# A written order for ScalarE, VectorE and GpSimd in a two-pair delta-rule scan, with its steps rearranged and two transfers on GpSimd's queue

## The chip, the cores and the metric

The kernel runs on one core of one Trainium2 chip. The metric is the device time of one execution in microseconds (us); the median of three runs of the kernel before is 2773.27 us. One execution was also taken by the hardware profiler, and its page and trace are what is read here. Engines: PE is TensorE's matmul side, PEld its weight loads, DVE is VectorE, ACT is ScalarE, POOL is GpSimd, SP is SyncE, which issues most transfers (DMAs).

## The reference

A two-layer decoder with a model width of 2048 and 272 tokens (16 learned meta tokens ahead of 256). Layer 0 is an RWKV-7 time mix followed by a SwiGLU; layer 1 is stick-breaking attention followed by a SwiGLU. The change touches the time mix alone, which has 32 heads of 64 channels:

```
r, k, v = xr @ w_r, xk @ w_k, xv @ w_v           # x* = h mixed with the token before
decay = exp(-exp(w)),  w from tanh(xw @ dec_w1) @ dec_w2
a = sigmoid(a_w0 + (xa @ a_w1) @ a_w2)
g = sigmoid(xg @ g_w1) @ g_w2
kk = k * k_k;  kk = kk / |kk| per head
k = k * (1 + (a - 1) * k_a)
for each token t, per head:
    sa    = state @ (-kk_t)
    state = state * d_t + sa (kk_t * a_t)^T + v_t k_t^T
    y_t   = state @ r_t
y = (y - mean) * rsqrt(var + GN_EPS) * gn_w + gn_b  # per head
out = ((y + sum(r * k * r_k) * v) * g) @ w_o
```

## The kernel before, in words

**Pairs and chunks.** Two heads fill the 128 partitions, so there are 16 head pairs (`Pair`). Tokens are cut into a chunk of 16 (meta) and four chunks of 64. In a chunk the recurrence becomes matrix products with the inverse of a unit triangular matrix. That inverse is made in three levels: the 16x16 diagonal blocks by substitution on GpSimd (`solve`, tiles As and Ts), then blocks of 32 (`left(16)`, `right(16)`), then of 64 (`left(32)`, `right(32)`). A level transposes the inverse so far (Tt into Tn, VectorE), multiplies it with the strict blocks (An times Tt into the bank yb, PE), masks that into Ys (VectorE), multiplies with Tn into the bank zb (PE, L1418) and adds zb into Tt (VectorE, L1422).

**The scan.** `scan` handles two pairs at a time and runs three stages of different pairs in one step d. A (pairs 2d, 2d+1) goes through the states: `states` and `update` (bank cb, L1470 and L1493), `output`, the group norm (`square`, `variance`, `log`, `norm`) and `gate` (bank gp, output o). B, the next two pairs, goes through `chunk0`, `scores`, `bonus`, `tokens`, the inverse, `values` (banks kv and k0), `apply` (tiles wa, X, Ah) and `trans` (bank rm). C, the two after, is prepared: `lora` makes the decays and keys (ld, L, P, Q, kk and the products AR, ARV, BK, B0), rk is the product for the bonus, and `negatives` makes the strict blocks (`neg`: bank b, tiles An and An0), sends them through DRAM scratch (s1, `diagonals`) into As and starts the solve. The step after stores Ts to scratch s2 and loads it back as Tt (`inverse`). Steps run from d = -2 to 7; d = 0 to 5 are alike and hold A, B and C. In d = 6 there is no C, in d = 7 neither B nor C.

**Fills.** Between the stages `f(k)` runs k accumulation steps of the projections w_r, w_v and, at the end, w_o. Such a step is three matmuls, since weights and activations are split in a high and a low part (`mm3k`, L200 to L202). The weight parts are made by ScalarE (whi, L228) and VectorE (wlo, L229), three pieces of four steps ahead. They are what keeps PE at work while the chains of the scan run on the other engines.

**What sets the order.** PE and SP run in the order in which the program is written. ScalarE, VectorE and GpSimd are ordered by a scheduler, but for a few instructions that `keep_in_program_order` holds: the transpose of the first level, the casts of weights and of the gates (`split_gates`, L202's wlo), and the copy in `split_low`.

**Other places that the steps below touch.** `head_sums` (L1193 to L1199) sums a tile over its head: it casts and splits it (tile hs, from rk or sq, the squares) and multiplies with a matrix of ones (vb, bv). The two products of kk with Q (B0, L1262; BK, L1263) are on VectorE, those of k with Q (L1264, L1265) on GpSimd. `load_norm` brings the keys' norms rn from DRAM (rkd), through SyncE's queue, as are all of `diagonals`' stores. rk takes the buffer of Q (`ALIAS`), Ah that of Tn. An0 and sq have one buffer. The norms of half of the keys come late, from `key_norm(1, late)` (L551 on: Ln, Exp and two table loads, L555); it is written behind `negatives` in d = -1, and the scheduler moves it ahead. The loads of h (L964), sixteen of 136 KB, go through GpSimd's queue in the last steps.

Of the kernel before, what the change touches and what calls it, by code (L numbers as in the profile page):

```python
# [11 lines left out]
F32 = mybir.dt.float32  # L12
# [25 lines left out]
ALIAS = {"kk": "ld", "rs20": "L", "rs21": "Q", "rk": "Q", "Ah": "Tn", "Mp": "Ys", "sq": "ta"}  # L38
# [94 lines left out]
class Builder:  # L133
# [240 lines left out]
    def time_mix(self):  # L374
# [15 lines left out]
        with ExitStack() as ctx:  # L390
# [6 lines left out]
            zero = zero.rearrange("p a b c t -> p (a b c t)")[:, :325]  # L397
            nc.gpsimd.memset(zero, 0.0)
            for i in range(2):
# [5 lines left out]
                for n, sides in (("s1", self.s1), ("s2", self.s2)):  # L405
                    z = self.dram.tile([10, 65, 64], F32, name=f"{n}_{i}", tag=f"{n}_{i}", bufs=1)
                    nc.scalar.dma_start(z.rearrange("s i t -> (s i t)").rearrange("(p x) -> p x", p=128),
                                        zero)
                    sides.append(z)
# [255 lines left out]
    def scan(self, sp):  # L665
# [25 lines left out]
        pairs[0].load_norm()  # L691
        for d in range(-2, NK // 2):
            A, B, C, N = two(d), two(d + 1), two(d + 2), two(d + 3)
            f = fill if C else lambda k: fill(k * 7 / 8)
# [892 lines left out]
```

## Time and profile before

| | |
|---|---|
| median of 3 runs | 2773.27 us (2773.12 to 2777.41) |
| profiled execution | 2768.93 us, span 2767.2 us |
| PE busy | 2664.3 us, 96% of the span (21030 matmuls) |
| PEld, DVE, ACT, POOL busy | 2484.6 (90%), 1780.0 (64%), 1468.1 (53%), 144.5 us (5%) |
| moved by DMA | 439.40 MB, 159 GB/s in the mean |
| steps d = 0 to 5 | begin at 245.9, 313.0, 378.7, 446.1, 511.9 and 577.6 us |
| steps d = 6 and 7 | begin at 643.9 and 700.9 us |

Times within the span are counted from its start. An instruction of the trace is shown by its start, its duration, engine, line, operation, output and input tiles, shapes, how many in a row, and in brackets how long its engine stood idle before it and which instruction released it. A group of waits shows the waiting matmul's tile and line, the releasing engine, tile and line, and the total, the count and the longest. A window shows length, busy time (and count) of PE, PEld, DVE, ACT and POOL, then the clock that TensorE was granted as a share of full speed, the busy share of the DMA engines and GB/s. The scan ends at about 760 us; the rest of the span is the feed-forward layers and the attention.

### The profile page before, as it was taken

What the parts mean: (1) busy time and instruction counts of PE and PEld (TensorE: products, weight loads), DVE (VectorE), ACT (ScalarE), POOL (GpSimd) and SP (SyncE); (2) the same over time, 40 slices, a digit from 0 to 9 for tenths busy, and PEclk for the clock granted to TensorE, in tenths of its full rate; (3) what the DMA queues carried; (4) which work ended last, traced back from release to release, by engine and by line L of the source; (5) the groups of instructions that cost most, each with busy time, mean ns of one, the idle gap of its engine ahead of it and who ended that gap; (6) DMA issues with size and microseconds to landing.
All of it is one profiled execution on the core that took longest, in us unless ns stands there. A gap on an engine that the chain in (4) does not pass through costs nothing.

```text
span 2767.2 us, 54183 instructions
## 1 busy us (share of the span) xinstructions
PE 2664.3 (96%) x21030; PEld 2484.6 (90%) x21030; DVE 1780.0 (64%) x3549; ACT 1468.1 (53%) x3030; POOL 144.5 (5%) x357
## 2 busy tenths in 40 slices
PE   9988888888999999999999999999999999999999
PEld 8887777778899999999999999988888888888888
DVE  7666555555665555555555876588776666666665
ACT  7764444444554444444444665477555455455553
POOL 0022222222000000000000000000000000000000
PEclk9999899999999999999999999999999999999999
DMA  6433333334455555555555555533555655655555
GB/s 228 139 113 99 85 92 86 86 89 118 136 175 176 167 185 175 166 186 171 169 184 167 181 171 171 175 123 114 175 186 179 200 189 176 198 189 179 197 180 177
DMA packets 186002, 439.40 MB, mean 159 GB/s; under 512 B 57328, under 2 KB 89232, under 8 KB 185744
## 3 DMA queue, kind: packets, MB, share of 16 engines
q1 hardware_dynamic: 184112, 432.41, 49.5%
q8 instruction: 165, 2.70, 0.4%
q0 software_dynamic: 768, 2.23, 0.3%
q10 hardware_dynamic: 864, 1.29, 0.1%
q14 instruction: 93, 0.76, 0.1%
HBM read 430.28 MB, written 5.58 MB: 158 GB/s over the span
## 4 chain that ended last, share of the span: by engine, by line
PE 87%; DVE 5%; ACT 3%; DMA 2%; issue 2%; POOL 1%; SPq 0%; DVEq 0%; ACTq 0%; POOLq 0%
PE mm L205 22%; PE mm L200 15%; PE mm L202 15%; PE mm L201 15%; PE mm L204 11%; DMA rn<-rkd 1%; PE lr L601 1%; PE mm L502 1%; DVE wlo L229 1%; PE zb L1418 1%; PE cb L1493 1%; PE z L1122 1%; PE lt L1135 0%; PE yb L1402 0%; POOL Tm L848 0%
## 5 line engine op out<-in xcount | busy, mean ns | idle before, releaser
L182 DVE TENSOR_TENSOR wlo<-raw,whi 128x512 fp32r<-128x512 f32 (+1 forms) x1432 | 968.1, 679 | 595.0 <-ACT whi L181 576.6
L181 ACT CAST whi<-raw 128x512 fp32r<-128x512 f32 (+1 forms) x1432 | 870.2, 610 | 841.9 <-PE mm L201 531.4
L200 PE MATMUL mm<-hl,whi 128*128 128x272 f32 x3328 | 968.3, 291 | 1.8 <-ACT hl L271 1.8
L202 PE MATMUL mm<-hl,wlo 128*128 128x272 f32 x3328 | 965.8, 290 | 0.3 <-DVE wlo L229 0.3
L201 PE MATMUL mm<-hl,whi 128*128 128x272 f32 x3328 | 963.3, 289 | 0.0
L205 PE MATMUL mm<-hl,whi 128*128 128x512 f32 x2624 | 919.8, 395 | 0.0
L204 PE MATMUL mm<-hl,wlo 128*128 128x256 f32 x2624 | 739.1, 282 | 0.0
L200 PEld LDWEIGHTS mm<-hl,whi 128*128 128x128 f32 x3328 | 630.3, 189 | 6.4 <-issue 2.8
L201 PEld LDWEIGHTS mm<-hl,whi 128*128 128x128 f32 x3328 | 635.5, 191 | 0.0
L202 PEld LDWEIGHTS mm<-hl,wlo 128*128 128x128 f32 x3328 | 630.5, 189 | 1.0 <-DVE wlo L229 0.7
L205 PEld LDWEIGHTS mm<-hl,whi 128*128 128x128 f32 x2624 | 492.9, 188 | 111.0
L204 PEld LDWEIGHTS mm<-hl,wlo 128*128 128x128 f32 x2624 | 494.9, 189 | 0.3
L229 DVE TENSOR_TENSOR wlo<-raw,whi 128x512 fp32r<-128x512 f32 (+1 forms) x154 | 103.8, 698 | 69.8 <-ACT whi L228 68.8
L228 ACT CAST whi<-raw 128x512 fp32r<-128x512 f32 (+1 forms) x154 | 88.2, 612 | 24.5 <-PE mm L201 14.1
L221 DVE TENSOR_TENSOR h<-h,mm 128x256 f32<-128x256 f32 (+1 forms) x224 | 93.9, 420 | 6.6 <-PE mm L205 6.0
L200 PE MATMUL mm<-hi,whi 128*128 128x272 f32 x256 | 79.4, 310 | 0.0
L214 ACT COPY c<-mm 128x256 f32<-128x256 f32 x104 | 38.8, 373 | 76.0 <-PE mm L205 76.0
L202 PE MATMUL mm<-hi,wlo 128*128 128x272 f32 x256 | 75.2, 294 | 0.3 <-DVE wlo L229 0.3
L201 PE MATMUL mm<-lo,whi 128*128 128x272 f32 x256 | 75.5, 295 | 0.0
L1418 PE MATMUL zb<-Ys,Tn 64*64 64x64 f32 x512 | 24.4, 256 | 42.3 <-DVE Tn L1394 40.9
L1418 PEld LDWEIGHTS zb<-Ys,Tn 64*64 64x64 f32 x512 | 21.7, 167 | 45.2 <-issue 42.3
L200 PEld LDWEIGHTS mm<-hi,whi 128*128 128x128 f32 x256 | 50.2, 196 | 2.9 <-issue 0.6
(301 smaller groups left out, 2427.9 us busy)
## 6 DMA issues: line engine op xcount, KB each, us to landing
raw<-w_gate SPq DMA_DIRECT2D x176, 512.0 KB
raw<-w_up SPq DMA_DIRECT2D x176, 512.0 KB
raw<-w_down SPq DMA_DIRECT2D x128, 512.0 KB
raw<-w_down SPq DMA_DIRECT2D x128, 192.0 KB
raw<-w_r SPq DMA_DIRECT2D x32, 512.0 KB
raw<-w_v SPq DMA_DIRECT2D x32, 512.0 KB
raw<-sb_w_k SPq DMA_DIRECT2D x32, 512.0 KB
raw<-sb_w_v SPq DMA_DIRECT2D x32, 512.0 KB
```

Of the source, the lines that this page charges most:

```text
L181: nc.scalar.copy(hi, part)
L182: nc.vector.tensor_tensor(lo, part, hi.bitcast(F32), ALU.subtract)
L200: mm(out, w[0], x[0], start=first, stop=False)
L201: mm(out, w[0], x[1], start=False, stop=False)
L202: return mm(out, w[1], x[0], start=False, stop=last)
L204: mm(out[:, :n], w[1], x[0], start=first, stop=False, skip_group_check=True)
L205: return mm(out, w[0], x[2], start=False, stop=last, skip_group_check=True)
L214: self.nc.scalar.copy(c, out[:, n:])
L221: self.nc.vector.tensor_tensor(h, h, out[:, c:c + n], ALU.add)
L228: self.cast = nc.scalar.copy(hi, part)
L229: nc.vector.tensor_tensor(lo, part, hi.bitcast(F32), ALU.subtract)
L1418: self.PE.matmul(zb[r, i * 64:i * 64 + 64], self.Tn[r, i], self.Ys[r, i], start=True, stop=True)
```

## The change

**Written order.** From d = -1 on, `in_order` chains every instruction of ScalarE, VectorE and GpSimd to the one written before it on the same engine. Only the splits of the outputs o stay free (`loose`). The calls of `keep_in_program_order` in these parts go.

**The step rearranged.** The numbers of fills between the stages change. B's inverse is fetched ahead of the bonus, and A's squares are summed between bonus and tokens. `lora` is cut in two: `decay` (matmuls, ld, L, ta, k2) stands ahead of the first inverse level, `keys` (P, Q, kk, AR, ARV, BK, B0, rk) behind it. The norm is cut as well: the exponent (`root`) stays early, the rest comes behind the first level, one pair behind `values` and one behind `left(32)`. `gate` moves from ahead of `left(32)` to behind `apply`; `split_gates` stays where it was, some fills ahead of `right(32)`. `negatives` moves four fills behind `right(32)`.

**Engines and queues.** The products of kk with Q go from VectorE to GpSimd, the square in the norm from VectorE to ScalarE, the product of y with the norm from VectorE to GpSimd. `load_norm` and the stores of An0 in `diagonals` go from SyncE's to GpSimd's queue. The scratch tiles s1 and s2 become one each for both pairs, so that one store carries Ts and one load As.

**Banks and buffers.** kv and k0 of the two pairs move from banks 0, 4 and 1, 5 to 0, 2 and 1, 3. yb of `left(32)` lies in banks 0 and 1 where C exists. The norm's factor lies in the tile that becomes o.

The first place is VectorE around the first inverse level of a like step. Before, the keys kk with all their products stand ahead of the transposes Tn, and the adds of zb into Tt come last:

```order
L1238 SCALAR_TENSOR_TENSOR kk<-kt,vecs,rn 128x272
L1274 TENSOR_TENSOR AR_5375<-mm,P 128x16
L1258 SCALAR_TENSOR_TENSOR AR_5375<-kk,P 128x16
L1259 SCALAR_TENSOR_TENSOR ARV<-kk,P 128x4x64
L1275 TENSOR_TENSOR ARV<-mm,P 128x4x64
L1261 SCALAR_TENSOR_TENSOR kk<-ta,kk 128x272
L229 TENSOR_TENSOR wlo<-raw,whi 128x512
L1262 TENSOR_TENSOR B_0_2017<-kk,Q 128x16
L1263 TENSOR_TENSOR BK<-kk,Q 128x2x2x64
L1394 STREAM_TRANSPOSE Tn<-Tt 128x256 x2
L1278 SCALAR_TENSOR_TENSOR rk<-mm,dv,k_5368 128x272
L1422 TENSOR_TENSOR Tt<-Tt,zb 128x256
```

The same place after; the second pair's transpose and its masked product Ys now come first, and the keys stand between them and the two adds:

```order
L1436 STREAM_TRANSPOSE Tn<-Tt 128x256
L1445 TENSOR_TENSOR Ys<-yb,consts 128x256
L1280 SCALAR_TENSOR_TENSOR kk<-kt,vecs,rn 128x272
L1300 SCALAR_TENSOR_TENSOR AR_6272<-kk,P 128x16
L1301 SCALAR_TENSOR_TENSOR ARV<-kk,P 128x4x64
L1303 SCALAR_TENSOR_TENSOR kk<-ta,kk 128x272
L1316 TENSOR_TENSOR AR_6272<-mm,P 128x16
L1317 TENSOR_TENSOR ARV<-mm,P 128x4x64
L1320 SCALAR_TENSOR_TENSOR rk<-mm,dv,k_6220 128x272
L1231 TENSOR_TENSOR hs<-rk,hs 128x272
L229 TENSOR_TENSOR wlo<-raw,whi 128x512
L1460 TENSOR_TENSOR Tt<-Tt,zb 128x256 x2
```

What moved: the transposes from behind the keys to ahead of them, the two products of kk with Q away from VectorE, and rk, the split of hs and a weight split to ahead of the adds.

The second place is ScalarE behind `neg`, where An is the copy of the strict 64x64 blocks and An0 (16x16) that of the meta chunk. Before:

```order
L1335 COPY An<-b_5718 128x128
L1335 COPY An<-b_5719 128x128
L1338 COPY An_5733<-b_5718 16x16 x2
L1335 COPY An<-b_5737 128x128
L1335 COPY An<-b_5736 128x128
L1198 CAST hs<-rk 128x272
L1338 COPY An_5751<-b_5736 16x16 x2
L228 CAST whi<-raw 128x512 x2
L1442 COPY X<-wa 64x2x128 x4
L228 CAST whi<-raw 128x512 x4
```

After, in the same stretch:

```order
L1377 COPY An<-b_5687 128x128
L1377 COPY An<-b_5688 128x128
L1380 COPY An_5702<-b_5687 16x16 x2
L1377 COPY An<-b_5705 128x128
L1377 COPY An<-b_5706 128x128
L1380 COPY An_5720<-b_5705 16x16 x2
L228 CAST whi<-raw 128x512 x2
L1480 COPY X<-wa 64x2x128 x4
L1230 CAST hs<-rk 128x272
L228 CAST whi<-raw 128x512 x4
```

What moved: the cast of rk, which stood ahead of the second pair's An0, now stands behind it and behind the copies X; the rest reads alike, but it is now fixed, so nothing passes a copy that waits.

The third place is GpSimd in the same step, where B is the part of a product for the meta chunk, BK that for the others, and the numbered k is k2. Before, the copy into Ts and the products of both pairs stand ahead of the first step of the solve (Tm, the last row), and no transfer is among them:

```order
L844 COPY Ts<-consts 80x256
L1234 TENSOR_SCALAR k_6258<-ta,vecs,dv 128x272
L1235 TENSOR_TENSOR k_6258<-k_6258,kt 128x272
L1264 TENSOR_TENSOR B_0_2017<-k_6258,Q 128x16
L1265 TENSOR_TENSOR BK<-k_6258,Q 128x2x128
L1234 TENSOR_SCALAR k_6438<-ta,vecs,dv 128x272
L1235 TENSOR_TENSOR k_6438<-k_6438,kt 128x272
L1264 TENSOR_TENSOR B_1_2027<-k_6438,Q 128x16
L1265 TENSOR_TENSOR BK<-k_6438,Q 128x2x128
L848 TENSOR_TENSOR Tm<-Ts,As 80x15
```

After, from the second pair's products to the copy into Ts with which the solve begins:

```order
L1304 TENSOR_TENSOR B_1_2025<-k_5528,Q 128x16
L1305 TENSOR_TENSOR BK<-k_5528,Q 128x2x128
L1306 TENSOR_TENSOR B_1_2025<-kk,Q 128x16
L1307 TENSOR_TENSOR BK<-kk,Q 128x2x2x64
L1560 TENSOR_TENSOR y<-y,o 128x272
L1236 DMA rn<-rkd 128x1x272
L867 DMA s_2015<-An_5702 16x16 x2
L867 DMA s_2015<-An_5720 16x16 x2
L875 COPY Ts<-consts 80x256
```

What moved here: L1306, L1307 and L1560 came from VectorE, the three rows of DMA from SyncE; they stand ahead of the solve.

The diff, cut to its core:

```diff
-            self.s1 = []
-            self.s2 = []
+            self.s1, self.s2 = (self.dram.tile([20, 65, 64], F32, name=n, tag=n, bufs=1)
+                                for n in ("s1", "s2"))
...
+            if d == -1:
+                mark = traced[-1]
...
             for x in B:
                 x.scores()
-            f(6 if A else 2)
+            if B:
+                self.inverse(B)
+            f(1)
             for x in B:
                 x.bonus()
+            for x in A:
+                x.square()
+            f(2 if A else 1)
             for x in B:
                 x.tokens()
-            if B:
-                self.inverse(B)
-            for x in A:
-                x.square()
+            f(4 if A else 1)
             for x in A:
                 x.variance()
             for x in A:
                 x.log()
             for x in A:
-                x.norm()
+                x.root()
+            f(3)
+            if C:
+                C[0].decay(2, 3)
+            f(3)
+            for x in B:
+                x.left(16)
+            if C:
+                C[0].keys()
+                C[1].load_norm()
+            f(6)
+            for x in B:
+                x.right(16)
+            f(2)
+            for x in B:
+                x.values()
+            if A:
+                A[0].norm()
+                if not C:
+                    A[1].norm()
             f(4)
             if C:
-                C[0].lora(2, 3)
+                C[1].decay(2, 3)
             f(4)
             for x in B:
-                x.left(16)
-            f(5)
-            for x in B:
-                x.right(16)
-            for x in B:
-                x.values()
+                x.left(32, bool(C))
             if C:
-                C[1].load_norm()
-            f(5)
-            if C:
-                C[1].lora(2, 3)
-            f(5)
+                C[1].keys()
+                if A:
+                    A[1].norm()
+                if N:
+                    self.load_low(N)
+                    N[0].load_norm()
+            f(3)
             self.split_gates(gates, A)
             f(4)
-            for x in A:
-                x.gate()
-            for x in B:
-                x.left(32)
-            f(7)
             for x in B:
                 x.right(32)
+            f(4)
             if C:
                 self.negatives(C)
             if d == -1:
                 key_norm(1, late)
-            f(8)
+            f(5)
             for x in B:
                 x.apply()
-            if N:
-                self.load_low(N)
-                N[0].load_norm()
-            f(8)
+            f(3)
+            for x in A:
+                x.gate()
+            f(5)
             for x in B:
                 x.trans()
-            f(8)
+            f(11)
+        self.in_order(traced, mark)
         fill(100)
...
+    def in_order(self, traced, mark):
+        start = next(k for k, i in enumerate(traced) if i is mark) + 1
+        kinds = mybir.EngineType
+        prev = {}
+        for i in list(traced[start:]):
+            if i.engine not in (kinds.Activation, kinds.DVE, kinds.Pool) or i.name in self.loose:
+                continue
+            if i.engine in prev:
+                self.tc.add_manual_dep(
+                    i, prev[i.engine].name,
+                    mybir.DependencyInfo(mybir.DependencyClass.NoSync, mybir.DependencyReason.DATA),
+                    reason="order")
+            prev[i.engine] = i
...
-                self.dq.dma_start(s1[r, 0:META, 4, 0:META], x.An0[HS[r]][:META])
-        for i, x in enumerate(two):
-            self.dq.dma_start(self.As[i * 40:i * 40 + 40], x.diag(self.s1[i]))
+                self.nc.gpsimd.dma_start(s1[r, 0:META, 4, 0:META], x.An0[HS[r]][:META])
+        self.dq.dma_start(self.As, Pair.diag(self.s1))
...
-        for i, x in enumerate(two):
-            self.dq.dma_start(x.diag(self.s2[i]), self.Ts[i * 40:i * 40 + 40])
+        self.dq.dma_start(Pair.diag(self.s2), self.Ts)
...
-        self.nc.sync.dma_start(self.rn, self.b.rkd[2 * self.p:2 * self.p + 2].unsqueeze(1).to_broadcast([2, 64, T]))
+        self.nc.gpsimd.dma_start(self.rn, self.b.rkd[2 * self.p:2 * self.p + 2].unsqueeze(1).to_broadcast([2, 64, T]))
...
-        V.tensor_tensor(self.B0[:, 0:META], kk[:, :META], Q[:, :META], ALU.mult)
-        V.tensor_tensor(par(BK, 0, 1), c4(kk), c4(Q), ALU.mult)
         E.tensor_tensor(self.B0[:, 32:32 + META], k2[:, :META], Q[:, :META], ALU.mult)
         E.tensor_tensor(par(BK, 1, 0), c4(k2), c4(Q), ALU.mult)
+        E.tensor_tensor(self.B0[:, 0:META], kk[:, :META], Q[:, :META], ALU.mult)
+        E.tensor_tensor(par(BK, 0, 1), c4(kk), c4(Q), ALU.mult)
...
-        kv = self.bank("kv", 0, 4)
-        k0 = self.bank("k0", 1, 5)
+        kv = self.bank("kv", 0, 2)
+        k0 = self.bank("k0", 1, 3)
...
-        if s == 16:
-            b.tc.keep_in_program_order(op)
-            yb = self.bank("yb", 0, 1)
-        else:
-            yb = self.bank("yb", 4, 5)
+        yb = self.bank("yb", 0, 1) if low else self.bank("yb", 4, 5)
...
     def log(self):
-        self.rs2 = self.t272(f"rs2{self.e}")
-        self.A.activation(self.rs2, self.vb, AF.Ln, bias=self.b.gneps)
+        self.out = self.b.kp.tile([128, T], F32, name="o", tag="kp")
+        self.A.activation(self.out, self.vb, AF.Ln, bias=self.b.gneps)
+
+    def root(self):
+        self.A.activation(self.out, self.out, AF.Exp, scale=-0.5)
 
     def norm(self):
...
-        V.tensor_tensor(sq, rs2, rs2, ALU.mult)
+        self.A.activation(sq, rs2, AF.Square)
         V.scalar_tensor_tensor(sq, vb, GN_EPS, sq, ALU.add, ALU.mult)
         V.scalar_tensor_tensor(rs2, sq, -3.0, rs2, ALU.add, ALU.mult)
-        V.tensor_tensor(y, y, rs2, ALU.mult)
-        V.scalar_tensor_tensor(y, y, self.vec("mgn"), self.bv, ALU.mult, ALU.add)
+        self.nc.gpsimd.tensor_tensor(y, y, rs2, ALU.mult)
...
     def gate(self):
         b = self.b
         w = self.wg
+        self.V.scalar_tensor_tensor(self.y, self.y, self.vec("mgn"), self.bv, ALU.mult, ALU.add)
```

More of the change, by code (lines that the diff above doesn't have):

```diff
@@ L37 @@
 CONST = {}
-ALIAS = {"kk": "ld", "rs20": "L", "rs21": "Q", "rk": "Q", "Ah": "Tn", "Mp": "Ys", "sq": "ta"}
+ALIAS = {"kk": "ld", "rk": "Q", "Ah": "Tn", "Mp": "Ys", "sq": "ta"}
 NRAW = 4
@@ L404, in time_mix @@
                 self.static.append(st)
[L405 to L409, printed above, removed]
+            for z in (self.s1, self.s2):
+                nc.scalar.dma_start(z.rearrange("s i t -> (s i t)").rearrange("(p x) -> p x", p=128),
+                                    zero)
             self.blk = [sp.tile([128, 128], F32R, name="blk", tag=f"blk{i}") for i in range(2)]
@@ L801, in split_low @@
         l = self.l2.tile([128, 512], F32R, name="w2l", tag="w2l", bufs=1)
-        self.tc.keep_in_program_order(self.nc.scalar.copy(h, self.low))
+        self.nc.scalar.copy(h, self.low)
         self.nc.vector.tensor_tensor(l, self.low, h.bitcast(F32), ALU.subtract)
@@ L819, in split_gates @@
         h, l = self.whl_pair(w)
-        self.tc.keep_in_program_order(self.cast)
         for i, x in enumerate(two):
@@ L1221, in lora, with keys @@
         V.tensor_tensor_scan(L, b.cst("reset"), ld, 0.0, ALU.mult, ALU.add)
-        ta = self.t272("ta")
+        self.L = L
+        self.ta = ta = self.t272("ta")
         A.activation(ta, za[:, :T], AF.Tanh, bias=self.vec("ha0"), scale=0.5)
+        self.k2 = k2 = self.t272("k2")
+        E.tensor_scalar(k2, ta, self.vec("k_a"), self.vec("oka"), ALU.mult, ALU.add)
+        E.tensor_tensor(k2, k2, kt, ALU.mult)
+    def keys(self):
+        b, p, V, A, nc = self.b, self.p, self.V, self.A, self.nc
+        E = LORA(nc)
+        kt, rn, L, ta, k2 = b.k[p], self.rn, self.L, self.ta, self.k2
         self.P = P = b.P
@@ L1386, in values, with left @@
         A.copy(self.KV0, k0[:, 0:64])
-    def left(self, s):
+    def left(self, s, low=True):
         b, V, PE = self.b, self.V, self.PE
```

24 lines of the change are left out of this document (13 added, 11 removed).

## The prediction

> **What bounds the kernel now.** I read the windows by stage first. In each the columns are the length, then the busy time and count of PE, its weight loads, VectorE, ScalarE and GpSimd, then the granted TensorE clock, DMA share and GB/s.
>
> ```profile
> 900.00:1000.00 100.00, 100.00 (x799) 100.00 (x798) 56.47 (x98) 43.44 (x76) 0.00 (x0) 1.00 0.54 175
> 446.00:512.00 66.00, 54.53 (x732) 50.14 (x732) 36.66 (x90) 30.66 (x82) 16.75 (x42) 0.92 0.34 90
> 644.00:701.00 57.00, 49.76 (x656) 45.60 (x654) 31.51 (x77) 25.11 (x61) 10.93 (x33) 0.91 0.38 119
> ```
>
> From 760 us on PE never stops and the change touches nothing there. In the scan PE is idle for 11 of 66 us and its clock falls. The other engines are half idle, so they are late, not full. Next come PE's own waits (total, times, longest), and the ends of one step.
>
> ```profile
> PE zb L1418 <- DVE Tn L1394: 40.9, 6, 6.9
> PE gp L202 <- DVE wlo L229: 18.3, 6, 3.7
> PE gp L200 <- ACT whi L228: 3.5, 6, 0.6
> ...
> 445.75 0.29 PE L201 MATMUL mm<-hl,whi 128*128 128x272 f32 x1
> 445.88 0.29 PE L202 MATMUL mm<-hl,wlo 128*128 128x272 f32 x1
> 446.10 0.29 PE L1470 MATMUL cb<-SC,WV 64*64 64x16 f32 x4
> ...
> 475.95 0.37 PE L1418 MATMUL zb<-Ys,Tn 64*64 64x64 f32 x2 [6.89 <-DVE Tn L1394]
> ...
> 511.94 0.29 PE L1470 MATMUL cb<-SC,WV 64*64 64x16 f32 x4
> ```
>
> Six like steps, 65.84 us each (446.10 to 511.94). In each PE waits 6.8 us at `right(16)` for the transposes and 0.6 + 3.05 us in `gate` for the gates' split: 10.45 us. A filling matmul takes 0.125 us, start to start. I count from a step's start; PE reaches the first wait at 22.96 (475.95 - 6.89 - 446.10). Behind each wait the clock falls:
>
> ```profile
> 476.00:478.00 2.00, 2.00 (x50) 2.00 (x52) 1.41 (x5) 0.94 (x2) 0.00 (x0) 0.50 0.03 8
> 478.00:480.00 2.00, 2.00 (x35) 1.88 (x32) 1.49 (x4) 1.51 (x5) 0.00 (x0) 0.50 0.23 45
> ...
> 490.00:492.00 2.00, 2.00 (x10) 1.93 (x10) 1.49 (x3) 0.00 (x0) 0.00 (x0) 0.59 0.75 256
> 492.00:494.00 2.00, 2.00 (x40) 1.82 (x40) 0.93 (x3) 0.00 (x0) 0.00 (x0) 0.56 0.65 203
> ```
>
> PE is busy at half clock for 4 us, then at 0.59 and 0.56 for 4: lost work of 2.0 + 1.7 = 3.7 us. A step without these waits would take 65.84 - 10.45 - 3.7 = 51.7.
>
> **Term 1, the first inverse level (faster).** VectorE's rows, then ScalarE's:
>
> ```profile
> 470.77 0.29 DVE L1220 TENSOR_SCALAR ld<-ld 128x272 f32<-128x272 f32 x1
> 470.98 0.41 DVE L1407 TENSOR_TENSOR Ys<-yb,consts 128x256 f32<-128x256 f32 x1
> 471.31 0.71 DVE L1221 TENSOR_TENSOR_SCAN L<-consts,ld 128x272 f32<-128x272 f32 x1
> ...
> 475.37 0.76 DVE L1394 STREAM_TRANSPOSE Tn<-Tt 128x256 f32<-128x256 f32 x2
> 476.06 0.45 DVE L1278 SCALAR_TENSOR_TENSOR rk<-mm,dv,k 128x272 f32<-128x272 f32 x1
> 477.10 0.42 DVE L1422 TENSOR_TENSOR Tt<-Tt,zb 128x256 f32<-128x256 f32 x1 [0.59 <-PE zb L1418]
> 477.44 0.44 DVE L1199 TENSOR_TENSOR hs<-rk,hs 128x272 fp32r<-128x272 f32 x1
> 477.79 0.68 DVE L229 TENSOR_TENSOR wlo<-raw,whi 128x512 fp32r<-128x512 f32 x1
> ```
> ```profile
> 460.22 0.65 ACT L1364 COPY G<-tb 128x256 f32<-128x256 f32 x2
> 460.75 0.43 ACT L1198 CAST hs<-sq 128x272 fp32r<-128x272 f32 x1
> 461.26 0.59 ACT L1367 COPY X<-tv 128x512 f32<-128x512 f32 x1
> 461.87 1.28 ACT L1510 ACT_TABLE_LOAD   x1
> ...
> 466.50 0.48 ACT L1219 ACTIVATE ld<-zw,dv 128x272 f32<-128x272 f32 x1
> ```
>
> VectorE holds the whole norm and the keys ahead of the transposes. The change puts both behind them; the second norm square goes to ScalarE, the product with y to GpSimd. Now `ld` gates everything. The bonus stands 15 fills (1.9 us) earlier, so the second `hs` cast starts at 460.75 - 446.10 - 1.9 = 12.75; behind it come 0.43, all four G and two X copies (2 x 0.65 + 2 x 0.59), a weight cast 0.52 and the 4.63 from table load to `ld`: 20.8, 0.4 later than now. VectorE then has `ld` until 21.3, the rest of a split 0.25, 0.29, 0.71, a split 0.6, and transpose and mask 0.38 + 0.41 for each pair: Ys at 23.95 and 24.7. As many fills lie ahead of `right(16)` as before (57), so PE comes at 22.96 and waits 1.1 us in place of 6.8.
>
> **Term 2, a new wait in `values` (slower).** `kv` and `k0` of the second pair move from banks 4 and 5 to 2 and 3, which hold both pairs' zb. PE may write them only when VectorE has added zb into Tt, and in the written order that add stands behind the keys, rk, hs and a split. Two prices come from here:
>
> ```profile
> 485.25 0.74 POOL L1265 TENSOR_TENSOR BK<-k,Q 128x256 f32<-128x256 f32 x1
> 485.86 0.50 DVE L1238 SCALAR_TENSOR_TENSOR kk<-kt,vecs,rn 128x272 f32<-128x272 f32 x1 [2.11 <-DMA rn<-rkd]
> ...
> 487.02 0.44 DVE L1261 SCALAR_TENSOR_TENSOR kk<-ta,kk 128x272 f32<-128x272 f32 x1
> ```
>
> From 24.7: kk to kk 1.6 (485.86 to 487.46); the two products moved to GpSimd 0.2 + 0.74, for which rk must wait since it takes Q's buffer; rk 0.45; ScalarE's cast 0.43; hs 0.44; the split 0.68; Tt 0.42: 29.7, and 30.1 for the second pair. PE has the second zb, six fills (0.75) and the first pair's kv behind 24.75, some 1.9 us by my estimate (the busy 4 us at half clock above hold both zb and both kv and fills besides), so 26.6. It waits 3.1 + 0.4 = 3.5 us. If my queue is too long by 3 us this is nothing; above, nothing in these rows reaches 6.
>
> **Term 3, the gates and `An0`.** The gates' split now lies long before `gp`: 3.65 us go. A late link comes instead. An0 has one buffer, so ScalarE's copy for the second pair waits until the first pair's stores land, and these leave through GpSimd's queue. In the written order the casts, X copies and rk's cast stand behind that copy.
>
> ```profile
> L964 POOL DMA_DIRECT2D h<-xT x16: 536/536/728, 634.9 to 643.5; - x16
> ...
> DMA to landing us min/median/max: 2.6/4.0/8.3
> ...
> 503.93 0.34 ACT L1338 COPY An<-b 16x16 f32<-16x16 f32 x2
> 504.29 1.14 ACT L228 CAST whi<-raw 128x512 fp32r<-128x512 f32 x2
> ```
>
> Before shows no store on GpSimd's queue. Above stands the slowest load there, 8.3 us; below, SyncE's same store, landed by 503.93. I take 2.6, the quickest load: these stores hold 1 KB. The Trainium skill, "DMA: Bandwidth & Descriptors" (Anatomy of one DMA), gives this queue a fixed cost of about 2.0 us; by that the sum would be 0.6 us a step better, and no run here shows it yet. From the start of `neg`: An0 at 1.2, second issue at 1.75, landed 4.35; copy 0.34 and two casts 1.14, 5.85; VectorE's split 0.68, two Ah 0.84, AR, ARV and rk 0.95, 8.3; cast and hs 0.87; then y, o, y, o at some 0.47: 11.0. `trans` needs gp's banks 4 and 5, so it waits for both o. PE has neg 1.1, wa 1.96, 39 fills 4.9 and gp 1.5: 9.5. Wait 1.5 us.
>
> **Term 4, the clock.** The wait of 3.5 us is about as long as those at the gates, so I charge a half-clock spell of 1.75. For 1.5 us this is near:
>
> ```profile
> 714.57 0.87 PE L1193 MATMUL vb<-hs,blk 128*128 128x272 f32 x2 [2.18 <-ACT hs L1198]
> ...
> 716.00:717.00 1.00, 1.00 (x6) 1.00 (x5) 0.68 (x2) 0.98 (x2) 0.00 (x0) 0.50 0.06 16
> ```
>
> A gap of 2.18 us is followed by half clock, so behind 1.5 us I charge half a spell, 0.9. Here the Trainium skill's page "TensorE: Matmul & The Clock Gate" (Why this matters for your kernels) says otherwise: no drop without an idle gap of over some 3 us. This row differs, so it enters only as a rival.
>
> **Sum of a step.** Gone: 10.45 + 3.7 = 14.15. New: 1.1 + 3.5 + 1.75 + 1.5 + 0.9 = 8.75. A step takes 60.4, that is 5.4 less; six of them 32.4.
>
> **The other steps.** Ahead of the six:
>
> ```profile
> 171.99 1.28 ACT L555 ACT_TABLE_LOAD   x1
> ...
> 181.25 0.72 PE L1328 MATMUL b<-BK,ARV 64*64 64x64 f32 x16 [3.86 <-DVE BK L1263]
> ...
> 658.31 0.74 POOL L1315 COPY Rh<-ARV 128x256 f32<-128x256 f32 x2
> ```
>
> The late key norm (two table loads, 1.28 each, and its Ln) now runs in a scheduled hole at 171.99, and the keys behind it make PE wait 3.86. Written, it stands behind `neg` of the next step: some 3 us saved in one place, some 4.5 spent in the other, where ScalarE's casts and VectorE's Ah queue behind An0 and those loads: -1.5. In the step without new keys (57 us now) the solve ends at 658.31, 14.4 after its start, since sixteen loads of h stand ahead of it on GpSimd; that stays. PE will come earlier to `left(16)` and wait there for Tt, so of its gaps some 4 us go and no more. At the end the product with y adds a hop through GpSimd: -1. The single store of Ts, the single load of As, and rn on GpSimd's queue I cost at nothing: the solve's 12 us and the six fills ahead of `keys` cover them; without that cover each would cost an issue, 0.54.
>
> Together 32.4 - 1.5 + 4 - 1 = 33.9. The profiled execution took 2768.93 (span 2767.2): 2735 by it. The median of the three runs is 4.3 higher, 2773.27, so I forecast 2739.
>
> **Rivals.**
>
> The clock stays up behind the short waits, as that page would have it. Each step keeps 1.75 + 0.9 = 2.65, six 15.9: 2723. For it: the first 1.1 us wait is too short to matter. Against: the 2.18 us gap. Chance 0.12.
>
> The new waits don't come: ScalarE and VectorE run ahead of what I strung together, so kv finds Tt added and An0 is not late. Then 3.5 + 1.75 + 1.5 + 0.9 = 7.65 more a step, 46: 2693. For it: both engines are busy half the step. Against: strict order, each link above has its row. Chance 0.15.
>
> GpSimd's stores land at the median of its loads, 4.0: the third term grows by 1.4 and its clock to the full 1.75, 2.3 a step, 14: 2753. Chance 0.13.
>
> **Slower or nothing gained:** they land as its slowest load, at 8.3. ScalarE stands for them, and casts, X, rk, both o and PE's `trans` behind it: 5.7 + 0.9, and 0.5 at `left(16)`, where As comes late too: 7.1 a step, 43: 2782. It cancels the gain at a landing of some 7.3 us. For it: ScalarE can't pass the blocked copy any more, as it did with rk's cast before 503.93. Against: 1 KB against loads of 136 KB, sixteen in flight. Chance 0.20, of which 0.08 end within 0.2% and 0.12 beyond.
>
> That the order isn't obeyed is no rival: the rows of the changed program stand as written.
>
> **How the numbers follow.** Forecast 0.40, the rivals 0.12, 0.15, 0.13 and 0.20. Faster by over 0.2% (5.5 us, about what a measurement of this kernel tells from no change): 0.40 + 0.12 + 0.15 + 0.13 = 0.80; within 0.08; slower 0.12. From 2698 to 2780 lies all but half of the second rival and most of the slow end: some 0.8.
>
> **What would show it.** Right: PE's waits in each step are zb for Ys near 1 us, `kv` for Tt near 3 and `rm` for o near 1.5; gp's wait is gone; steps of some 60 us; a half-clock spell behind kv. Term 2 is wrong if kv shows no wait on Tt; term 3 if rm shows none, or if ScalarE isn't idle before An0's second copy. The whole is wrong if PE waits for weight splits (wlo) in the fills, which I costed at nothing because casts lie three chunks ahead, or for Tt in every step.

## The result, and the profile after

The changed kernel takes 2749.88 us in the median of four runs (2747.76 to 2752.10), against 2773.19 of the kernel before. The ratio is 0.9915, 95% interval 0.9897 to 0.9932: faster by 0.85%, where 2739 us were forecast. The profiled execution took 2748.35 us with a span of 2746.6, so 20.6 us are to be found in the trace.

PE's waits after, in the columns of the list before (total, times, longest):

```profile
PE kv L1419 <- DVE Tt L1460: 18.6, 7, 2.9
PE rm L1489 <- DVE o L1570: 17.4, 12, 2.6
PE cb L1531 <- ACT S L1525: 11.1, 24, 0.6
PE zb L1456 <- DVE Ys L1445: 9.0, 7, 1.3
PE b L1370 <- POOL BK L1307: 6.5, 1, 6.5
PE gp L200 <- ACT An L1380: 6.1, 5, 1.4
```

The waits for Tn (40.9 us) and for the gates' split (21.8 us) are gone, but for 0.5 us. In their place stand the three links that the prediction named, zb and kv in nearly the forecast size and rm at twice it, and one at gp that it did not have. That one comes five times and not six. The waits at cb are not new (9.8 us in 22 before); the one at b lies ahead of the six steps. The like step that began at 446.10 before is this one after:

```profile
442.02 0.29 PE L1508 MATMUL cb<-SC,WV 64*64 64x16 f32 x4
...
466.23 1.34 PE L1456 MATMUL zb<-Ys,Tn 64*64 64x64 f32 x32 [1.28 <-DVE Ys L1445]
...
472.05 0.53 PE L1419 MATMUL kv<-X,G 64*64 64x64 f32 x10 [2.92 <-DVE Tt L1460]
...
493.11 0.39 PE L200 MATMUL gp<-hg0h,whi 128*128 128x272 f32 x1 [1.36 <-ACT An L1380]
...
499.35 0.43 PE L1489 MATMUL rm<-G,Ah 64*64 64x128 f32 x2 [2.59 <-DVE o L1570]
500.36 2.03 PE L1489 MATMUL rm<-G,Ah 64*64 64x128 f32 x30 [0.58 <-DVE o L1570]
508.54 0.29 PE L1508 MATMUL cb<-SC,WV 64*64 64x16 f32 x4
```

It lasts 66.52 us, against 65.84: nothing is gained in it. The starts of all steps give the account:

| stretch | before, us | after, us | gain | forecast |
|---|---|---|---|---|
| up to step 0 | 245.9 | 246.8 | -0.9 | -1.5 |
| steps 0 to 4 | 331.7 | 327.6 | 4.1 | 27.0 |
| step 5 | 66.2 | 60.5 | 5.8 | 5.4 |
| step 6 | 57.0 | 48.6 | 8.4 | 4 |
| step 7 and after | | | 3.2 | -1 |
| all | | | 20.6 | 33.9 |

Step 5 is what was forecast, 60.48 us against 60.4. Steps 0 to 4 take 65.0 to 66.5. Steps 0, 3 and 5 as windows:

```profile
246.83:311.90 65.07, 55.10 (x729) 50.42 (x728) 35.55 (x82) 31.18 (x84) 26.20 (x55) 0.95 0.37 98
442.02:508.54 66.52, 56.34 (x730) 51.60 (x729) 35.77 (x82) 31.08 (x84) 27.03 (x58) 0.92 0.34 92
574.44:634.92 60.48, 53.34 (x730) 49.03 (x729) 36.87 (x86) 35.47 (x96) 25.92 (x52) 0.97 0.36 95
```

PE is idle for 10.0, 10.2 and 7.1 us of them, and its clock is lower in the first two. What steps 0 to 4 have and step 5 has not are the loads for a pair after next: its rn, and the weights w of its second projection. ScalarE and GpSimd in step 3, at the stores of An0:

```profile
487.28 0.43 ACT L1377 COPY An<-b 128x128 f32<-128x128 f32 x2
492.71 0.35 ACT L1380 COPY An<-b 16x16 f32<-16x16 f32 x2 [4.99 <-DMA s<-An]
493.08 1.14 ACT L228 CAST whi<-raw 128x512 fp32r<-128x512 f32 x2
```
```profile
484.58 0.85 POOL L1236 DMA_DIRECT2D rn<-rkd  x1
487.39 1.02 POOL L867 DMA_DIRECT2D s<-An  x2 [1.96 <-ACT An L1380]
```

And in step 5, ScalarE's copy and PE's wait behind it:

```profile
621.86 0.35 ACT L1380 COPY An<-b 16x16 f32<-16x16 f32 x2 [2.02 <-DMA s<-An]
```
```profile
628.49 0.43 PE L1489 MATMUL rm<-G,Ah 64*64 64x128 f32 x2 [0.91 <-DVE o L1570]
```

The same copy waits 4.99 us with rn under way and 2.02 without. PE pays for these 3 us with 1.36 at gp and 1.7 more at rm, and then with its clock. The windows behind kv and behind rm in step 3:

```profile
472.00:474.00 2.00, 1.95 (x25) 1.84 (x26) 0.93 (x2) 1.33 (x6) 0.00 (x0) 0.60 0.61 116
474.00:476.00 2.00, 2.00 (x11) 2.00 (x11) 1.48 (x3) 0.77 (x2) 0.70 (x1) 0.55 0.48 186
500.00:502.00 2.00, 1.64 (x30) 1.63 (x30) 2.00 (x6) 0.00 (x0) 1.76 (x4) 0.50 0.09 16
502.00:504.00 2.00, 2.00 (x13) 1.68 (x8) 2.00 (x9) 0.00 (x0) 1.69 (x5) 0.50 0.68 238
504.00:506.00 2.00, 2.00 (x11) 2.00 (x10) 0.65 (x1) 0.00 (x0) 1.69 (x5) 0.50 0.44 113
506.00:508.00 2.00, 2.00 (x16) 2.00 (x15) 0.00 (x0) 0.00 (x0) 1.58 (x6) 0.87 0.75 253
```

Busy time times the missing share of the clock: 1.95 x 0.40 + 2.00 x 0.45 = 1.7 us behind kv, and 0.8 + 1.0 + 1.0 + 0.3 = 3.1 us behind rm. The spell behind rm is that long in step 3 alone; in steps 0, 1, 2 and 4 it takes 3.4 us at half clock, so 1.7 us are lost, and in step 4 the one behind kv is the long one (6.8 us at half clock). In step 5, with 0.91 and 0.59 at rm, the windows 628 to 630 and 630 to 632 have the full clock. The first pair's two stores of An0, for which the copy waits, landed 1.7 and 2.1 us after their issue in step 5, and 4.6 to 5.2 us in steps 0 to 4. The second pair's, for which no copy waits, mostly took 1.5 to 1.6 in both.

Step 6, without new keys, before and after:

```profile
643.90:700.90 57.00, 49.76 (x655) 45.60 (x654) 31.61 (x77) 25.20 (x61) 11.03 (x33) 0.91 0.39 119
```
```profile
634.90:683.50 48.60, 45.87 (x654) 42.02 (x654) 29.85 (x71) 24.11 (x59) 11.85 (x32) 1.00 0.40 123
```

PE's idle time falls from 7.2 to 2.7 us and its clock stays up; PE waits for Tt nowhere in it.

### The profile page after: what moved, and what is told of

Its sections match the earlier page's. It is cut to its first block, busy times and chain, and to the rows that moved or that the text cites. A ratio compares the mean times of both kernels' runs of the same rounds, so it can differ in the third digit from the quotient of the medians.

```text
span 2746.6 us, 54212 instructions
## 1 busy us (share of the span) xinstructions
PE 2659.4 (97%) x21030; PEld 2477.4 (90%) x21030; DVE 1769.2 (64%) x3485; ACT 1469.8 (54%) x3044; POOL 216.1 (8%) x453
## 4 chain that ended last, share of the span: by engine, by line
PE 85%; DVE 5%; ACT 4%; issue 3%; DMA 1%; POOL 1%; SPq 0%; DVEq 0%; ACTq 0%; POOLq 0%
PE mm L205 22%; PE mm L200 15%; PE mm L202 14%; PE mm L201 14%; PE mm L204 11%; PE lr L599 1%; PE mm L500 1%; DVE wlo L229 1%; DMA s<-An 1%; ACT whi L228 1%; DVE G L1353 1%; PE cb L1531 1%; PE z L1154 1%; PE cb L1515 0%; PE lt L1167 0%
## 5 line engine op out<-in xcount | busy, mean ns | idle before, releaser
L463 ACT ACTIVATE u<-hn,vecs 128x272 f32<-128x272 f32 x96 | 44.3, 513 | 7.5 <-DVE hn L493 6.4
L201 PEld LDWEIGHTS mm<-lo,whi 128*128 128x128 f32 x256 | 48.2, 188 | 0.0
```

The source lines that it names most:

```text
L201: mm(out, w[0], x[1], start=False, stop=False)
L463: A.mul(u, hn[k][:, :T], self.vec(f"mu{i}", k))
```

## The experiments

The question was why five steps gained nothing, and whether the other links are what the prediction took them for. A fill is here, as in the diff, one step that `f` counts, three matmuls or 0.375 us at full clock; the prediction counts the matmuls. Ratios are to the kernel before, measured in the same runs; the changed kernel has 0.9915.

**rn's load behind apply.**

```diff
-                if N:
-                    self.load_low(N)
-                    N[0].load_norm()
...
                 x.apply()
+            if N:
+                self.load_low(N)
+                N[0].load_norm()
```

> The loads for the pairs after next (the second projection's weights on SyncE's queue, rn on GpSimd's) go back behind apply; all else as changed (2749.9 us, steps 0 to 4 of 65 to 66.5 us, step 5 of 60.5). Theory Q (rn, 136 KB, stands on GpSimd's queue ahead of An0's 1 KB stores, which therefore land late): in steps 0 to 4 ScalarE waits 2.0 us instead of 5.0 for its second An0 copy, gp's wait of 1.4 goes, rm's falls from 3.2 to 1.5, and no half clock follows; 5 us in each of five steps, 2725 us. Theory L (the loads as such, on whichever queue, slow the stores): the same. Rival F (the stores take that long by themselves, and step 5 is short because no pair follows it): steps stay at 65, 2750 us.

Measured: 2732.02 us, ratio 0.9867 (0.9851 to 0.9883). The steps from the second on take 60.5 to 62.1 us. ScalarE's wait for the second An0 copy is 2.1 us in four of six steps, 3.6 and 3.8 in the others. Rival F falls. The gain over the changed kernel is 13 us by the ratios and 18 by the medians, not 25: An0's wait did not go everywhere, and rm still waited 2.3 to 2.6 us in three steps, one of them with An0's wait at 2.1. In the two steps with 3.6 and 3.8 us no rn is on its way, but a packet of 16 KB on the queue q8 (instruction) is, beside the stores; whether that is the cause was not tried. The run moved two loads at once and does not tell rn from the weights.

**rn on SyncE's queue.**

```diff
-        self.nc.gpsimd.dma_start(self.rn, ...
+        self.nc.sync.dma_start(self.rn, ...
```

> Only rn goes back to SyncE's queue, at the same place; An0's stores stay on GpSimd's. Theory Q (rn ahead on the same queue delays the stores): ScalarE's wait for An0 falls to 2.0 us, steps 0 to 4 to some 60.5 us, 2725 us. Theory L (the loads as such compete for the DMA engines): the wait stays at 4 us or more, 2745 to 2752 us.

Measured: 2731.99 us, 0.987 (0.985 to 0.989); ScalarE's wait is 2.0 to 2.1 us in five steps and 3.5 in the sixth. Theory L falls as far as it meant the second projection's weights, which stayed where they were. It looked like theory Q. But SyncE issues rn earlier: at 351.75 in the second step, 6 us ahead of An0's stores, where GpSimd issued it 2.8 us ahead of them. Queue and moment had both changed.

**An0's stores on SyncE's queue, rn still on GpSimd's.**

```diff
-                self.nc.gpsimd.dma_start(s1[r, 0:META, 4, 0:META], x.An0[HS[r]][:META])
+                self.dq.dma_start(s1[r, 0:META, 4, 0:META], x.An0[HS[r]][:META])
```

> An0's stores go back to SyncE's queue, one buffer, all else as changed (2749.9 us; with rn off GpSimd's queue 2732 us; with two buffers for An0 2712.5 us). Theory Q (GpSimd's queue with rn ahead is what delays them): ScalarE's wait for the second An0 copy falls to some 2 us and the time to 2732 us. Rival (on SyncE's queue they stand behind the two stores of An, 64 KB each, and the weights w, which landed in 4.8 to 5.0 us in the median): the wait stays at 4 us or more, 2745 us or more.

Measured: 2750.05 us, 0.9927 (0.9913 to 0.9942), no change. ScalarE's waits for the stores from the second step on:

```profile
ACT An L1380 <- DMA s<-An: 23.3, 5, 5.4
```

The last of the five, 3.1 us, is step 5's, without rn. So part of the wait is SyncE's own, which issues the four stores of a pair one after the other, 0.6 us each, and some 2 us come with rn. Theory Q looks wrong: the stores are late on a queue that rn isn't on. But they stand behind other transfers there, so this run alone does not rule it out.

**rn on SyncE's queue, but just ahead of the stores.**

```diff
-                    N[0].load_norm()
...
+            if N:
+                N[0].load_norm()
             if C:
                 self.negatives(C)
...
-        self.nc.gpsimd.dma_start(self.rn, ...
+        self.nc.sync.dma_start(self.rn, ...
```

> As changed, one buffer for An0 and its stores on GpSimd's queue, but rn on SyncE's queue and issued just ahead of An's stores there. With rn on SyncE's queue some 3 us earlier the time was 2732 us; with An0's stores off GpSimd's queue and rn on it, 2750 us, so the order within GpSimd's queue is not the cause. Theory C (rn in flight at that moment slows all stores, whichever queue carries it): ScalarE's wait for An0 is 4 us or more, 2745 to 2752 us. Rival (only what GpSimd's queue carries is slow to move): the wait is 2 us, 2732 us.

Measured: 2754.51 us, 0.9955 (0.9941 to 0.997), 2.5 us above the expected range, with ScalarE's wait at up to 5.8 us. The transfers' landing in the middle steps of this kernel, then of the one with rn on SyncE's queue and early (rows: tiles, queue, count, KB, median us):

```profile
s<-An SPq DMA_DIRECT2D x16, 64.0 KB, 4.7
s<-An POOLq DMA_DIRECT2D x16, 1.0 KB, 4.1
```
```profile
s<-An SPq DMA_DIRECT2D x16, 64.0 KB, 2.4
s<-An POOLq DMA_DIRECT2D x16, 1.0 KB, 1.7
```

With rn on its way at that moment the stores of both queues are slow, whichever queue carries rn; with rn early or late both are quick. Theory C holds, and theory Q falls: An0's stores are late on GpSimd's queue while rn is on SyncE's. The weight load of 512 KB that runs beside them is not enough to slow them: it is issued 2.2 us ahead of An0's first store in step 5 and in the kernel with rn early as well. What in rn slows them was not tried. In steps 0 to 4 of the changed kernel the first pair's An0 stores land 0.2 to 0.5 us behind rn (in step 3 at 492.25 and 492.61, rn at 492.07). And rn is a long transfer on few engines: its packets run from 486.2 to 491.7, and its queue keeps 11.5% of the 16 DMA engines busy meanwhile, so less than two of them. That the stores have a part on the same engines and wait for it there would fit both, but no run spread rn over more engines.

**Two buffers for An0.**

```diff
-BUFS = {n: 2 for n in "ARV BK AR0 G An Tt X BV0 Tn Ys Rh S KV0 WV0 y hs".split()}
+BUFS = {n: 2 for n in "ARV BK AR0 G An An0 Tt X BV0 Tn Ys Rh S KV0 WV0 y hs".split()}
```

> An0 gets two buffers, so that ScalarE's copy for the second pair waits for no store; the stores are as slow as they are. Theory (the one buffer carries the delay of the stores to ScalarE, and the written order carries it on to casts, X, rk, o and PE): gp's wait goes, rm's falls to below 1 us in all six steps, no half clock behind it; 5.5 us in five steps and 1 in the sixth, 2721 us. Rival (casts and copies are late for another reason, above all the wait of X for Ah behind the weight splits): rm still waits 2 us or more, 2740 to 2750 us.

Measured: 2712.53 us, 0.979 (0.9765 to 0.9815), some 35 us below the changed kernel by the ratios. The stores are as late as ever (4.5 to 4.7 us in the median in steps 0 to 4), but neither ScalarE nor gp waits for them, and rm next to nothing:

```profile
PE kv L1419 <- DVE Tt L1460: 18.4, 7, 2.9
...
PE rm L1489 <- DVE o L1570: 1.3, 6, 0.2
```

All six steps take 58.9 to 60.3 us. The gain is 9 us more than was expected; 4.8 of it lie ahead of step 0 (246.8 to 242.0). The one buffer carried the delay.

**Shared banks for kv and k0.**

```diff
-        kv = self.bank("kv", 0, 2)
-        k0 = self.bank("k0", 1, 3)
+        if not self.e:
+            b.kvk0 = b.bank(0, "kv"), b.bank(1, "k0")
+        kv, k0 = (x[:, self.e * 256:self.e * 256 + 256] for x in b.kvk0)
```

> kv of both pairs lies in halves of bank 0 and k0 of both in bank 1, so that kv of the second pair no longer takes a bank that holds zb; all else as changed (2749.9 us), An0 with its one buffer. Theory T2 (kv waits 2.9 us only for the bank, and its half clock costs 1.7): kv's wait goes, decay's zw in bank 2 waits some 0.7 us, 4 us in each of six steps and 2 in the others, 2724 us. Rival (the add into Tt is late for all: left(32) or zw then waits the same 2.9 us): 2744 us or more.

Measured: 2752.49 us, 0.9936 (0.9919 to 0.9952), no gain. The bank was not the whole link. ScalarE, then PE, around kv in the second step:

```profile
339.29 0.42 ACT L1230 CAST hs<-rk 128x272 fp32r<-128x272 f32 x1 [4.27 <-DVE rk L1320]
339.62 1.13 ACT L228 CAST whi<-raw 128x512 fp32r<-128x512 f32 x2
340.66 0.74 ACT L1426 COPY X<-kv 64x256 f32<-64x256 f32 x2
```
```profile
341.45 0.54 PE L1420 MATMUL kv<-X,G 64*64 64x64 f32 x10 [3.03 <-ACT X L1426]
```

In the shared bank the second kv waits for ScalarE's copy of the first, and that stands behind the cast of rk. VectorE's add had stood behind rk as well: both engines are held by the same product. With both this and two buffers the time was that of the two buffers alone:

> Two buffers for An0 and the shared banks for kv and k0 together. Theory (the two late links are separate and each costs what it does alone): 2712.5 - 26 = 2687 us, with no wait of PE above 1.5 us in the like steps and no clock below 0.95 in them. Rival (they cover each other: what PE gains at kv it gives back at rm or gp): 2700 us or more.

Measured: 2713.72 us, 0.9795 (0.9781 to 0.981). As a test of the bank it is inconclusive, since one wait took the other's place.

**right(16) four fills earlier, with two buffers for An0.**

```diff
-            f(6)
+            f(2)
             for x in B:
                 x.right(16)
-            f(2)
+            f(6)
```

> Two buffers for An0 (2712.5 us), and right(16) four fills earlier (2 and 6 fills around it instead of 6 and 2), so that the adds into Tt are written ahead of rk, hs and the split that follow the sixteenth fill. The run with shared banks moved the wait at kv from VectorE's add to ScalarE's copy of the first kv, both behind the cast of rk. Theory T2 (the queue behind rk makes kv wait): kv's 2.9 us go, zb's wait grows from 1.3 to 2.8 since PE comes 1.5 us sooner; the half clock moves from behind kv to behind zb; 1.4 us a step, 2703 us. Rival (the keys' five instructions make the add late, rk has no part): kv still waits 2 us or more, 2715 us or more.

Measured: 2706.91 us, 0.9779 (0.9758 to 0.9801). kv's wait is gone and zb's is what was expected:

```profile
PE zb L1456 <- DVE Ys L1445: 16.8, 6, 2.8
```

kv's wait alone does not decide, since PE also comes to the second kv later: some 5.7 us behind the start of zb instead of 2.9 (447.12 - 444.22 in step 3 with two buffers alone). VectorE's rows do. The start of the keys and the adds in step 3, with two buffers alone, then here:

```profile
444.66 0.65 DVE L1280 SCALAR_TENSOR_TENSOR kk<-kt,vecs,rn 128x272 f32<-128x272 f32 x1
449.57 0.75 DVE L1460 TENSOR_TENSOR Tt<-Tt,zb 128x256 f32<-128x256 f32 x2
```
```profile
442.01 0.65 DVE L1280 SCALAR_TENSOR_TENSOR kk<-kt,vecs,rn 128x272 f32<-128x272 f32 x1
443.71 0.75 DVE L1460 TENSOR_TENSOR Tt<-Tt,zb 128x256 f32<-128x256 f32 x2
```

The adds start 1.7 us behind the keys' first row instead of 4.9. So 3.2 us of their delay were the queue behind that: the keys' last two products, rk, the cast and split of hs, and the weight split. The steps fall from 58.9 to 60.3 to 58.2 to 59.4 us; the interval overlaps that of the two buffers alone. It is the fastest kernel of the study, some 61 us below the one before and 38 below the changed one by the ratios.

**Products of kk back on VectorE, with two buffers for An0.**

```diff
-        E.tensor_tensor(self.B0[:, 0:META], kk[:, :META], Q[:, :META], ALU.mult)
-        E.tensor_tensor(par(BK, 0, 1), c4(kk), c4(Q), ALU.mult)
+        V.tensor_tensor(self.B0[:, 0:META], kk[:, :META], Q[:, :META], ALU.mult)
+        V.tensor_tensor(par(BK, 0, 1), c4(kk), c4(Q), ALU.mult)
```

> Two buffers for An0 (2712.5 us), and the products of kk with Q back on VectorE. Theory (the move to GpSimd is about even: VectorE gets 0.9 us more ahead of rk, but rk no longer waits 0.6 us for GpSimd): kv waits 2.9 to 3.3 us, the one wait of 6.3 us ahead of the six steps falls to 4; 2709 to 2716 us. Rival (the move is worth the 0.9 us twice a step): 2721 us or more.

Measured: 2713.01 us, 0.9801 (0.9783 to 0.982): the move of the products is worth nothing that can be measured. The wait ahead of the six steps stayed, 6.0 us instead of 6.3, so its cause is not the move to GpSimd.

**The written order, by itself and taken away.** The chain left out of the changed kernel:

```diff
-        self.in_order(traced, mark)
```

> The chain of the written order is left out, so that the scheduler orders ScalarE, VectorE and GpSimd again (without the few fixed places that before had); the step's new order of writing, the queues and banks stay. Theory (the written order is what carries An0's delay on, and the rearranged step brings the rest): rk's cast and the weight casts pass the blocked copy, rm waits under 2 us; but the keys may pass the transposes again, and zb wait 3 to 6 us. The two nearly cancel: 2740 to 2765 us. Rival (the order itself brings the whole gain of 23 us): 2770 us or more. Rival (the order only costs): 2725 us or less.

Measured: 2757.06 us, 0.9956 (0.9938 to 0.9973), with 53.5 us of waits of PE for ScalarE's copies of the states, up to 8.8 at once. The time is in the range of the theory, but not for its reason: zb, where 3 to 6 us were expected, does not wait. The same with two buffers and shared banks:

> As the run with two buffers and shared banks, but without the chain of the written order: the scheduler orders ScalarE, VectorE and GpSimd. It tells what the written order is worth once nothing in it blocks. Without it and with both blocks in place the time was 2757 us, with it 2749.9. Theory (the order holds the transposes, the states' copies and the adds in front, and the scheduler put others ahead of the states' copies, on which PE waited up to 8.8 us): 2735 us or more, 50 us slower than with the order. Rival (the order was worth the 7 us seen and no more): 2695 us.

Measured: 2761.99 us, 0.9968 (0.9957 to 0.9979). And the chain put into the kernel before, with nothing else:

```diff
+        self.in_order(traced, mark)
         fill(100)
```

> The kernel before with nothing but the chain of the written order. The changed kernel without the chain took 2757 us. Theory (the order pays only together with the rearranged step, since the order as written before has norm and keys ahead of the transposes just as the scheduler had): zb's wait of 6.7 us stays or grows, 2765 to 2800 us. Rival (the order by itself brings much of the gain): 2760 us or less.

Measured: 2800.93 us, 1.0123 (1.0103 to 1.0143), 0.9 us above the expected range, with zb's wait at up to 5.7 us and the steps at 71 to 73. zb's wait fell a little where it was to stay or grow; new are waits for the casts of the squares (vb, 14.8 us in 15). ScalarE waits 3.1 to 4.7 us for An0's stores here as well. The largest group of PE's waits in each of the three:

```profile
PE cb L1530 <- ACT S L1524: 53.5, 30, 8.8
```
```profile
PE cb L1531 <- ACT S L1525: 42.0, 30, 7.0
```
```profile
PE zb L1441 <- DVE Ys L1430: 36.8, 8, 5.7
```

By the ratios the written order costs 34 us on the old step, is worth 11 on the new one, and 48 once An0 no longer blocks (and kv has the shared banks). What a scheduler could have passed, the blocked copy, was what held the order's gain back.

## Why the prediction was right or wrong, point by point

**What bounds the kernel:** right. The two waits went, and nothing changed after 760 us: from the last matmul of gp to the end of the span both kernels take 2040.9 us.

**Term 1, the first inverse level:** right. PE came to `right(16)` at 22.93 us of the step (466.23 - 1.28 - 442.02) and waited 1.28, where 22.96 and 1.1 were forecast (its rows add up to 1.0: 23.95 - 22.96).

**Term 2, the wait in `values`:** right in place and size: 2.92 us where 3.5 were forecast, and the second kv began at 30.03 where 30.1 was worked out. The shared banks showed that rk, and not the bank alone, is what PE waits for; the earlier `right(16)` put the adds 3.2 us further ahead, and the wait went.

**Term 3, An0:** the chain was right and its price failed. From the start of `neg` to the second copy of An0 the forecast had 4.35 us; step 5 shows 4.15 (621.86 - 617.71), and there rm waited 0.91 + 0.59 = 1.5, as said. Two errors cancel in that: the second store was issued 2.3 us behind the start, not 1.75, and landed in 1.7, not 2.6. But in steps 0 to 4 the copy came at 7.44. The steps that failed are two: "I take 2.6, the quickest load: these stores hold 1 KB", and "rn on GpSimd's queue I cost at nothing". rn's cover was looked for in its own readers (the fills ahead of `keys`) and not in what it meets: the change puts it some 3 us ahead of the stores, and 136 KB in flight take the stores that the copy waits for from some 2 to 5 us. In the sum this is gp's 1.1 to 1.4 us, which it did not have, 1.7 more at rm, and the clock.

**Term 4, the clock:** the charge behind kv (1.75) met 1.7 in five of six steps; step 4 had a double spell there. Half a spell behind 1.5 us was too much for step 5, which had none, and too little for steps 0 to 4, where it cost 1.7 in four and 3.1 in step 3 instead of 0.9. That the clock stays up behind waits of 1.5 us, as the rival had it, is what step 5 shows; behind those of 2.6 and 2.9 in this kernel it does not. Neither is a rule by length: with rn's load behind apply, 0.98 + 0.58 us at rm is followed by half clock in step 2, and 2.51 + 0.59 in step 3 is not.

**The sum of a step:** 5.4 forecast, 5.8 in step 5, 0.8 in the mean of the five others. It fits the best of the six and was multiplied by six. That it meets step 5 to 0.1 us is partly luck: the terms came to 7.4 there instead of 8.75 (kv 0.6 and the clock 0.9 less, zb 0.2 more), and two waits at cb of 0.57 each, which the forecast did not have, made most of that good.

**The other steps:** Up to step 0 the size was right. `neg`'s waiting matmuls start 3.3 us earlier (177.97 against 181.25) and 4.2 us are lost again until step 0, where 3 and 4.5 were said. But the wait for BK did not go: it grew from 3.86 to 6.46 us, while one of 4.2 us ahead of it for a weight cast (zw) went. So the 3 us were met, but not by the wait that was to go, and that is luck; what holds BK up there stays open, since moving the products back left 6.0. "PE will come earlier to `left(16)` and wait there for Tt" failed. With `neg` 17.2 us ahead of step 6 instead of 13.7 the solve ended 10.9 us into step 6 (645.79, start of the copy behind it), not 14.4, and Tt was there. Step 6 gave 8.4 us instead of 4, and step 7 and after gave 3.2 where 1 was to be lost, since the waits for the squares' casts (2.18 us and its clock) went too. These 8.6 us hide part of the 22.9 that the five steps fell short by.

**The rivals:** the one with stores landing at 4.0 us is nearest in time (2753), though the landing that counts was 4.6 to 5.2. But it would cost 2.3 us a step and the five steps fell 4.6 short: gp was not in it, the wait at rm grew by 1.7 and not 1.4, and steps 3 and 4 each had a double spell. The slow end did not come: at a landing of 5 us the steps still gained a little, and the break-even of 7.3 was put too high, since they gained 0.8 only (with the rival's own 0.5 at `left(16)` it would have been 6.9). That the new waits don't come was wrong. That the clock stays up was wrong for kv.

## What to carry to other kernels

An order written by hand is as good as its latest link: before it is fixed, look for every copy into a single buffer that only a transfer sets free, and give it a second buffer. Price a moved load also against the transfers that it will meet, not only against its own readers. And where steps are taken as alike, ask which of them lacks a load or a stage; the one that lacks it points at the cause already in the first profile.

## What the runs showed of the hardware

The half clock is not decided by the length of a wait alone. In the kernel with rn's load behind apply, kv waits 2.91 us in one step and 2.92 in the next. The two rows, then three windows of 3.41 us around each:

```profile
341.40 0.51 PE L1419 MATMUL kv<-X,G 64*64 64x64 f32 x10 [2.91 <-DVE Tt L1460]
...
403.22 0.51 PE L1419 MATMUL kv<-X,G 64*64 64x64 f32 x10 [2.92 <-DVE Tt L1460]
```
```profile
336.60:340.02 3.42, 1.89 (x37) 1.53 (x33) 2.19 (x8) 0.66 (x2) 1.71 (x3) 1.00 0.00 0
340.02:343.43 3.41, 2.03 (x31) 1.96 (x32) 2.19 (x5) 2.90 (x10) 0.00 (x0) 1.00 0.69 45
343.43:346.84 3.41, 3.41 (x49) 3.26 (x50) 3.29 (x6) 1.90 (x5) 2.27 (x3) 1.00 0.58 211
...
398.04:401.46 3.42, 2.26 (x44) 1.90 (x42) 2.35 (x7) 0.29 (x1) 1.87 (x4) 1.00 0.00 1
401.46:404.87 3.41, 1.65 (x28) 1.59 (x29) 2.40 (x5) 2.90 (x10) 0.00 (x0) 1.00 0.35 52
404.87:408.28 3.41, 3.41 (x17) 3.41 (x17) 2.34 (x5) 2.12 (x6) 1.19 (x2) 0.50 0.51 180
```

Behind the first the clock stays at 1.00, behind the second it falls to 0.50. What differs is how the wait falls on these windows, which are not chosen freely: between 200 and 760 us of all fourteen traces the granted clock changes only at moments that lie whole multiples of 3.413 us apart. The first wait leaves PE idle for 1.53 and 1.38 us in two such windows, the second for 1.16 and 1.76. Of the windows at full clock, none of the 1761 with less than 1.1 us of idle time was followed by half clock, all 133 with 1.9 us or more were, and 31 of the 171 in between. Idle time in a window at half clock prolongs the spell: with 0.6 us or more of it all 55 were followed by another, with under 0.2 none of 148. In step 3 of the changed kernel the second wait at rm, 0.58 us, lies in a window that is at half clock (499.70 to 503.12), and the next is at half clock too.

The Trainium skill, "TensorE: Matmul & The Clock Gate" (Part 1: The HAM clock gate), describes a free-running window of activity of some 3.4 us. These traces agree, with 3.413 us. A wait near 3 us is thus a risk of a spell, by its place, and not a fixed price.
